# All weight subtractions on VectorE, under a list schedule that knows of the port that VectorE and GpSimd share

## The chip, the cores and the metric

The kernel runs on one core of a Trainium2 chip. Its five engines are TensorE (PE in the views, its weight loads apart as PEld), VectorE (DVE), ScalarE (ACT), GpSimd (POOL) and SyncE (SP), which issues all the DMAs. The metric is the device time of one execution in microseconds, lower being better.

## What is computed

Two transformer-like blocks on 256 tokens of width 1024, all in float32:

```python
h = x
h = h + 0.5 * swiglu(rmsnorm(h), ffn1)                 # 1024 -> 2816 -> 1024
h = h + concat(window_attention(n), gla(n)) @ w_out    # n = rmsnorm(h), one w_in
h = h + 0.5 * swiglu(rmsnorm(h), ffn2)
h = h + sigmoid(rmsnorm(h) @ w_ple) * rmsnorm(p @ w_proj)
for layer in range(2):
    mix = mlstm_and_gated_delta(u) if layer == 0 else hgrn2(u)   # u = rms_norm(h)
    h = h + rms_norm(mix)
    h = h + rms_norm(conv_ffn(rms_norm(h)))            # 1024 -> 2 x 2816 -> 1024
return h
```

The weights are some 200 MB, each is read once, and each is multiplied with all 256 tokens.

## The kernel before

**Three matmuls for one product.** TensorE multiplies in the type float32r. So that little precision is lost, each operand is split in two: `hi` is the operand rounded to float32r, `lo` is the operand minus `hi`. A product is then the sum of three matmuls: x_hi by w_hi, x_lo by w_hi, x_hi by w_lo.

**The weight pipeline** (`halves`, L578 to L600). Weights arrive in half chunks of 128 x 1024 numbers (512 KB). One DMA on SyncE's queue brings a half chunk into one of 3 `raw` buffers. ScalarE rounds it into one of 6 `hi` buffers (L455). Two subtractions of 128 x 512 make the `lo` buffer, also one of 6 (L423). Only when these three have read it is `raw` free for the next DMA, and a `hi` or `lo` buffer is free when the matmuls that read it are done. The string `LOPAT` names the engine of the four subtractions of a chunk, V for VectorE and P for GpSimd.

**The stages.** Most of the time goes to four feed-forward networks. Their inner loop has groups of 256 hidden channels: two chunks of up-weights stand still in TensorE while the tokens move past (96 matmuls of 256 columns, `row_units`), VectorE and ScalarE make the 256 hidden channels (`row_fin`, or `up_fin` with a convolution), and one chunk of down-weights moves past them (24 matmuls of 512 columns, `down`). Between the networks lie three mixers and some normalisations, with chains of small operations.

**What sets the order.** `Plan` records every instruction with its engine, an assumed duration and its operands, and then simulates a list schedule at build time: on each engine the ready instruction with the highest priority goes next, within the buffers that are free (`forward`). A second pass takes its priorities from a schedule that is made backwards from the end. What comes out is one fixed queue for each engine, which the chip then works through in order, with semaphores. The assumed durations are in `tt`, `ts`, `stt`, `act`, `copy` and, for TensorE, in `pec`. So a duration that is changed there changes no instruction, only the queues. In the schedule of before the engines are independent of each other apart from data and buffers.

**What shares an engine with the subtractions.** GpSimd also does the elementwise products with `eng=TTX` (one for each 256 hidden channels, and several in the mixers) and the powers of the normalisations. VectorE does nearly all else that is elementwise.

Of the kernel before, what the change touches and what calls it, by code (L numbers as in the profile page):

```python
# [14 lines left out]
P = 128  # L15
# [33 lines left out]
LOPAT = "VVVP"  # L49
# [16 lines left out]
class Plan:  # L66
    """Records instructions, then issues them in the order of a list schedule: per engine the
    ready instruction with the longest way to the end first, within the tiles that are free.
    Every pair that touches the same bytes, one of them writing, keeps its recorded order."""

    ENGS = ("PE", "ACT", "DVE", "POOL", "SP")
    # from the end of one instruction to the start of one that needs it (ns)
    WAIT = {"PE": (0, 197, 197, 224, 200), "ACT": (260, 143, 142, 170, 200), "DVE": (256, 198, 127, 155, 200),
            "POOL": (203, 75, 60, 96, 200), "SP": (2000,) * 5}
    TICK, TICK_COLS = 3413.0, 3060  # the PE clock is halved after a tick with fewer columns
# [7 lines left out]
    def tile(self, tag, shape, dt=F32, bufs=1, keep=999):  # L83
        """A tile that lives from its first to its last use, in one of the tag's `bufs` places."""
# [47 lines left out]
    def add(self, alts, outs, ins, func=None, cols=0.0):  # L132
        """alts: the ways to do it, each (engine, ns, function that issues it)."""
        i = len(self.ops)
        if self.places is not None:
            self.ops.append(alts)
            return
# [4 lines left out]
        for key, m, q in rd:  # L142
            keys.add(key)
            bank = self.masks[key][1] == 0  # reads of one PSUM bank by two engines do not overlap
            deps.update(j for j, m2, q2, w in self.hist[key]
                        if (w or bank and [x[0] for x in self.ops[j][0]] + engs != 2 * engs[:1]) and m & m2 and q & q2)
# [15 lines left out]
    def order(self):  # L162
        """The best of a few list schedules: the first by the way to the end, the next ones by the
        latest starts of a schedule from the end backwards that prefers what ended last before."""
# [31 lines left out]
    def lat(self, i, j, e=None):  # L196
        """From the end of i (on e) to the start of j."""
        return self.WAIT[e or self.ops[i][0][0][0]][self.ENGS.index(self.ops[j][0][0][0])]

    def backward(self, when):  # L200
        """Latest starts (negative, 0 the end) with each engine doing one thing at a time."""
# [33 lines left out]
    def forward(self, rank, prio):  # L235
# [14 lines left out]
        free = dict.fromkeys(self.WAIT, 0.0)  # L250
        tset = "silu_and_others"
# [3 lines left out]
        def safe(tag, ks):  # L255
            """Whether the rest could still run in recorded order if `ks` got their places now."""
# [13 lines left out]
        def start(i):  # L270
            """Earliest start by data and tiles; None while a tile has no place."""
# [17 lines left out]
        def later(i, e, t):  # L289
            """Whether another engine would be done with i clearly before e."""  # L290
            end = t + next(x[1] for x in ops[i][0] if x[0] == e)
            return any(max(ready[i], free[x[0]]) + x[1] + ALT < end for x in ops[i][0] if x[0] != e)
        for _ in range(n):
            best = None
            for e, c in cand.items():
                el = []
                for i in c:
                    t = start(i)
                    if t is not None and not (len(ops[i][0]) > 1 and later(i, e, max(t, free[e]))):
# [39 lines left out]
            free[e] = fin[i] = t + c  # L339
            when[i] = (t, fin[i])  # L340
# [25 lines left out]
class Kern:  # L366
    def __init__(self, plan, a, tap):
        self.plan, self.nc, self.a, self.tap = plan, plan.nc, a, tap
        self.phase = 0
        self.pieces = PIECES  # of the first load of weights  # L370

# [43 lines left out]
    def tt(self, out, a, b, op, eng="DVE"):  # L415
        n = self.fsz(out)

        def way(eng):
# [4 lines left out]
            return eng, c, lambda: self.ew(eng).tensor_tensor(out=out, in0=a, in1=b, op=op)  # L423
        self.plan.add([way(x) for x in eng.split("|")], [out], [a, b])

    def ts(self, out, a, s1, s2=None, op0=ALU.mult, op1=None, eng="DVE"):
# [5 lines left out]
        self.plan.add([(eng, c, lambda: e.tensor_scalar(out=out, in0=a, scalar1=s1, scalar2=s2, op0=op0, **kw))], [out],  # L432
                      [a] + [x for x in (s1, s2) if hasattr(x, "tensor")])

    def stt(self, out, a, s, b, op0, op1, accum=None):
        self.plan.add([("DVE", 69 + 1.04 * self.fsz(out) + 62 * hasattr(s, "tensor"),
                        lambda: self.nc.vector.scalar_tensor_tensor(out=out, in0=a, scalar=s, in1=b, op0=op0, op1=op1, accum_out=accum))],  # L437
# [19 lines left out]
    def copy(self, out, a, eng=None):  # L457
        n = self.fsz(out)
        ways = {"DVE": ("DVE", 69 + (1.04 if self.ps_(out, a) else 0.53) * n,
                        lambda: self.nc.vector.tensor_copy(out, a)),  # L460
# [21 lines left out]
    def pec(l, r):  # L482
# [6 lines left out]
        if r.dtype == F32:  # L489
            return 2 * max(m / 1.2, 2.5 + n / 1.2), n / 1.2 * 2  # L490
        return max(m / 1.2, 2.5 + n / 2.4), n / 2.4
# [1424 lines left out]
```

## Time and profile before

| | |
|---|---|
| time, median of 3 runs | 1327.42 us (1326.01 to 1330.7) |
| span of the profiled execution, which is the only time known of it | 1328.2 us |
| TensorE matmuls busy | 1263.0 us, 95% |
| VectorE busy | 874.1 us, 66% |
| ScalarE busy | 675.2 us, 51% |
| GpSimd busy | 495.3 us, 37% |
| mean rate of the DMAs | 158 GB/s |

The profile is that of one execution. Busy time counts an instruction from its start to its end, and the ends overlap on pipelined engines, so TensorE at 95% doesn't say that TensorE works at its best rate 95% of the time. [...]

### The profile page before, as it was taken

The page shows a single profiled execution, that of the slowest core. Times are in us where ns is not written, and L with a number is a line of the kernel's source. Part 1 is how long each engine was busy: PE and PEld are TensorE (multiplying, and loading weights), DVE is VectorE, ACT ScalarE, POOL GpSimd, SP SyncE. Part 2 cuts the span into 40 slices and gives each one's busy share as a digit, 9 for nine tenths or more (in the row PEclk, how much of TensorE's full clock was granted, in tenths as well). Part 3 has the DMA queues.
Part 4 walks back from the last instruction along what each step waited for, and adds up shares of the span by engine and source line. Part 5 has one row for each costly group of instructions (what it writes and reads, how often), then busy time and mean ns, then how long its engine had stood idle before and what let it go on. Part 6 is the DMA issues. An engine that isn't in the chain of part 4 may idle for free.

```text
span 1328.2 us, 21657 instructions
## 1 busy us (share of the span) xinstructions
PE 1263.0 (95%) x8180; PEld 1110.6 (84%) x8180; DVE 874.1 (66%) x1434; ACT 675.2 (51%) x1126; POOL 495.3 (37%) x435
## 2 busy tenths in 40 slices
PE   7999999899999999999999989999899999999998
PEld 7899987567889998788877788999699777899896
DVE  5656566766655666759456867666867557766765
ACT  5444445544464344547445565555643255555554
POOL 3433333533243333225213333333334643333332
PEclk9999999899999999999999999999998899999999
DMA  8655554216455555542223554555643045555552
GB/s 277 204 191 181 181 177 144 97 57 203 148 173 175 184 180 186 178 142 68 96 96 111 189 170 162 173 190 180 200 149 128 17 143 174 174 177 188 173 177 98
DMA packets 61034, 209.52 MB, mean 158 GB/s; under 512 B 7409, under 2 KB 9602, under 8 KB 60802
## 3 DMA queue, kind: packets, MB, share of 16 engines
q1 hardware_dynamic: 60930, 208.14, 47.9%
q8 instruction: 64, 1.05, 0.3%
q14 instruction: 40, 0.33, 0.1%
HBM read 207.07 MB, written 1.05 MB: 157 GB/s over the span
## 4 chain that ended last, share of the span: by engine, by line
PE 53%; DVE 18%; DMA 13%; ACT 7%; issue 5%; POOL 4%; SPq 0%; DVEq 0%; ACTq 0%; POOLq 0%
PE psa L496 51%; DVE lo L423 10%; ACT hi L455 5%; DMA raw<-in_cf_u 4%; DMA raw<-in_w_ffn 4%; DVE big L437 3%; POOL lo L423 2%; DMA raw<-in_cf_d 2%; PE psa L507 2%; DVE big L423 2%; DMA raw<-in_w_out 1%; DMA raw<-in_w_ple 1%; DMA raw<-in_w_cB 1%; DVE g L423 1%; POOL sml L423 1%
## 5 line engine op out<-in xcount | busy, mean ns | idle before, releaser
L423 DVE TENSOR_TENSOR lo<-raw,hi 128x512 fp32r<-128x512 f32 (+1 forms) x567 | 469.0, 858 | 277.2 <-ACT hi L455 276.7
L455 ACT ACTIVATE hi<-raw 128x1024 fp32r<-128x1024 f32 x381 | 393.3, 1046 | 392.6 <-PE psa L496 271.9
L423 POOL TENSOR_TENSOR lo<-raw,hi 128x512 fp32r<-128x512 f32 (+1 forms) x189 | 302.5, 1601 | 570.3 <-ACT hi L455 534.0
L496 PE MATMUL psa<-xh,lo 128*128 128x256 f32 x1568 | 449.6, 287 | 12.3 <-DVE lo L423 11.4
L496 PE MATMUL psa<-xh,hi 128*128 128x256 f32 x1568 | 448.5, 286 | 12.0 <-ACT hi L455 9.2
L496 PE MATMUL psa<-xl,hi 128*128 128x256 f32 x1568 | 443.8, 283 | 0.0
L496 PEld LDWEIGHTS psa<-xh,lo 128*128 128x128 f32 x1568 | 298.4, 190 | 21.4 <-DVE lo L423 21.2
L496 PEld LDWEIGHTS psa<-xh,hi 128*128 128x128 f32 x1568 | 298.8, 191 | 20.6 <-ACT hi L455 10.3
L496 PEld LDWEIGHTS psa<-xl,hi 128*128 128x128 f32 x1568 | 298.3, 190 | 7.5 <-DVE xl L437 0.2
L496 PE MATMUL psa<-hi,halfr 128*128 128x512 f32 x720 | 205.9, 395 | 2.5 <-ACT halfr L455 2.0
L496 PE MATMUL psa<-hi,xh 128*128 128x512 f32 (+1 forms) x368 | 146.0, 416 | 1.1 <-ACT xh L455 1.1
L496 PEld LDWEIGHTS psa<-hi,halfr 128*128 128x128 f32 x720 | 124.8, 188 | 23.9 <-ACT halfr L455 3.7
L496 PE MATMUL psa<-lo,xh 128*128 128x512 f32 (+1 forms) x368 | 141.2, 401 | 2.0 <-DVE lo L423 1.9
L496 PE MATMUL psa<-hi,xl 128*128 128x512 f32 (+1 forms) x368 | 139.7, 417 | 3.3 <-DVE xl L423 3.2
L423 POOL TENSOR_TENSOR big<-big 128x256 f32<-128x256 f32 (+1 forms) x88 | 81.4, 926 | 97.5 <-ACT big L455 66.0
L496 PE MATMUL psa<-lo,halfr 128*128 128x512 f32 x360 | 114.0, 393 | 0.6 <-DVE lo L423 0.6
L496 PEld LDWEIGHTS psa<-big,big 128*128 128x128 f32 (+10 forms) x752 | 88.4, 180 | 24.8 <-issue 10.8
L496 PE MATMUL psa<-big,big 128*128 128x128 f32 (+13 forms) x752 | 103.8, 275 | 5.0 <-DVE big L423 2.2
L496 PEld LDWEIGHTS psa<-lo,xh 128*128 128x128 f32 x368 | 71.0, 193 | 19.2 <-DVE lo L423 4.5
L496 PEld LDWEIGHTS psa<-hi,xl 128*128 128x128 f32 x368 | 69.5, 194 | 18.8 <-DVE xl L423 6.8
L496 PEld LDWEIGHTS psa<-hi,xh 128*128 128x128 f32 x368 | 71.0, 193 | 14.8 <-ACT xh L455 2.7
L496 PEld LDWEIGHTS psa<-lo,halfr 128*128 128x128 f32 x360 | 67.6, 188 | 17.4 <-DVE lo L423 2.4
(166 smaller groups left out, 1058.9 us busy)
## 6 DMA issues: line engine op xcount, KB each, us to landing
raw<-in_w_ffn SPq DMA_DIRECT2D x131, 512.0 KB, 4.5
raw<-in_cf_u SPq DMA_DIRECT2D x88, 512.0 KB, 4.1
raw<-in_cf_d SPq DMA_DIRECT2D x44, 512.0 KB, 4.2
raw<-in_w_in SPq DMA_DIRECT2D x16, 512.0 KB, 4.2
raw<-in_w_abB SPq DMA_DIRECT2D x16, 512.0 KB, 4.2
raw<-in_w_cA SPq DMA_DIRECT2D x16, 512.0 KB, 3.9
raw<-in_w_cB SPq DMA_DIRECT2D x16, 512.0 KB, 4.1
raw<-in_w_abA SPq DMA_DIRECT2D x12, 512.0 KB, 4.6
```

What stands on the lines that cost most here:

```text
L423: return eng, c, lambda: self.ew(eng).tensor_tensor(out=out, in0=a, in1=b, op=op)
L437: lambda: self.nc.vector.scalar_tensor_tensor(out=out, in0=a, scalar=s, in1=b, op0=op0, op1=op1, accum_out=accum))],
L455: self.plan.add([("ACT", c, lambda: self.nc.scalar.activation(out, a, f, scale=scale, **kw))], outs, ins, SETS.get(f))
L496: return [self.nc.tensor.matmul(o, l, r, start=st, stop=sp) for o, l, r, st, sp in lst]
L507: self.plan.add([("PE", 2.5 + P / 1.2, lambda: self.nc.tensor.transpose(out, a, idn))], [out], [a, idn], cols=P * 2)
```

## The change

One letter of `LOPAT` moves the last subtraction of each chunk, 189 of 756, from GpSimd to VectorE. In the list schedule each way to do an instruction gets a fourth field: whether it holds the port that VectorE and GpSimd share. It is set for elementwise instructions of two inputs without an operand in PSUM, on either engine, and for VectorE's copies and scalar operations between buffers in SBUF. An instruction with the field set starts, in the simulated schedule, no earlier than the last such instruction ended, on whichever of the two engines. And `pec` and `tp` assume other durations for matmuls: 120 ns where they had 109 for 256 columns of float32r, and 230 where they had 216 for 512 columns. The comments and docstrings of the file are gone as well, and the rest of the text is the same.

```diff
-LOPAT = "VVVP"
+LOPAT = "VVVV"
...
     def add(self, alts, outs, ins, func=None, cols=0.0):
         i = len(self.ops)
+        alts = [x if len(x) == 4 else (*x, False) for x in alts]
...
         free = dict.fromkeys(self.WAIT, 0.0)
+        port = 0.0
...
-            return any(max(ready[i], free[x[0]]) + x[1] + ALT < end for x in ops[i][0] if x[0] != e)
+            return any(max(ready[i], free[x[0]], port if x[3] else 0.0) + x[1] + ALT < end for x in ops[i][0] if x[0] != e)
...
                     t = start(i)
+                    if t is not None and any(x[3] for x in ops[i][0] if x[0] == e):
+                        t = max(t, port)
...
             free[e] = fin[i] = t + c
+            if ops[i][0][way][3]:
+                port = fin[i]
...
-            return eng, c, lambda: self.ew(eng).tensor_tensor(out=out, in0=a, in1=b, op=op)
+            return eng, c, lambda: self.ew(eng).tensor_tensor(out=out, in0=a, in1=b, op=op), op != ALU.pow and not self.ps_(a, b)
...
-        self.plan.add([(eng, c, lambda: e.tensor_scalar(out=out, in0=a, scalar1=s1, scalar2=s2, op0=op0, **kw))], [out],
+        self.plan.add([(eng, c, lambda: e.tensor_scalar(out=out, in0=a, scalar1=s1, scalar2=s2, op0=op0, **kw),
+                        eng == "DVE" and not self.ps_(out, a))], [out],
...
-                        lambda: self.nc.vector.scalar_tensor_tensor(out=out, in0=a, scalar=s, in1=b, op0=op0, op1=op1, accum_out=accum))],
+                        lambda: self.nc.vector.scalar_tensor_tensor(out=out, in0=a, scalar=s, in1=b, op0=op0, op1=op1, accum_out=accum),
+                        not self.ps_(a, b))],
...
-                        lambda: self.nc.vector.tensor_copy(out, a)),
+                        lambda: self.nc.vector.tensor_copy(out, a), not self.ps_(out, a)),
...
         if r.dtype == F32:
-            return 2 * max(m / 1.2, 2.5 + n / 1.2), n / 1.2 * 2
-        return max(m / 1.2, 2.5 + n / 2.4), n / 2.4
+            if l.shape[0] <= 64:
+                return 2 * (m + n) / 1.2, n / 1.2 * 2
+            return 2 * max(4 + m / 1.2, 2.5 + n / 1.2), n / 1.2 * 2
+        return max(4 + m / 1.2, 9.5 + 0.4316 * n), n / 2.4
...
-        self.plan.add([("PE", 2.5 + P / 1.2, lambda: self.nc.tensor.transpose(out, a, idn))], [out], [a, idn],
+        self.plan.add([("PE", 4 + P / 1.2, lambda: self.nc.tensor.transpose(out, a, idn))], [out], [a, idn],
```

The first place where the queues differ in a way that the prediction uses is VectorE in the inner loop of the first feed-forward network. `lo<-raw,hi` is a subtraction of weights, `big<-psa,half` the scaling of 256 new channels from PSUM, `halfr` the low half of those channels. Before, over half a group:

```order
L423 TENSOR_TENSOR big_145<-psa_117,half_110 128x512
L423 TENSOR_TENSOR lo_104<-raw_102,hi_129 128x512 x2
L423 TENSOR_TENSOR halfr_122<-big_143,halfr_121 128x256
L423 TENSOR_TENSOR lo_130<-raw_106,hi_123 128x512
L423 TENSOR_TENSOR lo_119<-raw_114,hi_129 128x512 x2
L423 TENSOR_TENSOR big_146<-psa_137,half_110 128x512
```

And after:

```order
L430 TENSOR_TENSOR big_145<-psa_131,half_110 128x512
L430 TENSOR_TENSOR lo_119<-raw_102,hi_107 128x512 x2
L430 TENSOR_TENSOR halfr_122<-big_143,halfr_121 128x256
L430 TENSOR_TENSOR lo_116<-raw_114,hi_123 128x512 x2
L430 TENSOR_TENSOR lo_104<-raw_106,hi_107 128x512 x2
L430 TENSOR_TENSOR lo_119<-raw_102,hi_107 128x512 x2
L430 TENSOR_TENSOR lo_104<-raw_114,hi_123 128x512 x2
L430 TENSOR_TENSOR halfr_128<-big_144,halfr_127 128x256
```

Subtractions that stood alone, because GpSimd had the other half, are now pairs.

The second place is GpSimd's queue at the same part of the program. Before:

```order
L423 TENSOR_TENSOR lo_130<-raw_102,hi_129 128x512
L423 TENSOR_TENSOR lo_116<-raw_114,hi_103 128x512
L423 TENSOR_TENSOR big_144<-big_144 128x256
L423 TENSOR_TENSOR big_145<-big_145 128x256
L423 TENSOR_TENSOR lo_130<-raw_106,hi_123 128x512
```

And after, where `big<-big` is the product of 256 channels with their gates:

```order
L430 TENSOR_TENSOR big_144<-big_144 128x256
L430 TENSOR_TENSOR big_145<-big_145 128x256
L430 TENSOR_TENSOR big_146<-big_146 128x256
L430 TENSOR_TENSOR big_147<-big_147 128x256
L430 TENSOR_TENSOR big_148<-big_148 128x256
```

The subtractions have left it, and only the products remain there.

The third place is VectorE in the second mixer, where the triangular inverse begins. `c_lmf` and `c_ident` are tables in SBUF, `psa` is PSUM. Before:

```order
L423 TENSOR_TENSOR big_141<-big_111,c_lmf_66 128x512
L423 TENSOR_TENSOR big_90<-c_ident_62,big_91 128x512
L423 TENSOR_TENSOR lo_124<-raw_102,hi_118 128x512
L423 TENSOR_TENSOR big_149<-c_ident_62,psa_131 128x512
L423 TENSOR_TENSOR lo_130<-raw_114,hi_107 128x512
L423 TENSOR_TENSOR big_152<-big_152,psa_105 128x128x2
L423 TENSOR_TENSOR big_142<-c_ident_62,big_141 128x512
```

And after:

```order
L430 TENSOR_TENSOR big_146<-c_ident_62,big_141 128x512
L445 SCALAR_TENSOR_TENSOR big_89<-psa_125,s_15_239,big_132 128x128
L430 TENSOR_TENSOR big_91<-c_ident_62,psa_136 128x512
L445 SCALAR_TENSOR_TENSOR big_89<-psa_125,s_15_239,big_132 128x128 x3
L445 SCALAR_TENSOR_TENSOR big_92<-psa_109,s_15_239,big_151 128x128 x4
L445 SCALAR_TENSOR_TENSOR big_143<-psa_137,s_15_239,big_72 128x128 x4
L430 TENSOR_TENSOR big_91<-big_91,psa_136 128x128x2
L430 TENSOR_TENSOR big_147<-big_89,c_lmf_66 128x512
```

Operations that read PSUM have moved ahead of those with two inputs in SBUF, and the subtractions of weights have moved behind this stretch.

## Rows read from the trace of the kernel before

**Rows 1.** The page: busy time, share of the span and number of instructions of each engine, and the shares of the span on the chain that ended last.

```profile
PE 1263.0 (95%) x8180; PEld 1110.6 (84%) x8180; DVE 874.1 (66%) x1434; ACT 675.2 (51%) x1126; POOL 495.3 (37%) x435
...
PE 53%; DVE 18%; DMA 13%; ACT 7%; issue 5%; POOL 4%; SPq 0%; DVEq 0%; ACTq 0%; POOLq 0%
```

**Rows 2.** The waits of TensorE's weight loads (each matmul has one ahead of it) over the whole span: for whom, us in total, how often, the longest.

```profile
PEld psa L496 <- DVE lo L423: 28.2, 58, 1.4
PEld psa L507 <- DVE big L437: 16.5, 15, 3.7
...
PEld psa L496 <- DVE xl L423: 7.0, 9, 2.0
PEld psa L496 <- POOL lo L423: 4.3, 8, 1.7
```

**Rows 3.** The instructions that write or read the tile `lo`: number, shortest, median and longest in ns; and from the same view who waited for them (us, times).

```profile
L423 DVE TENSOR_TENSOR lo<-raw,hi x567: 426/691/1815, 7.0 to 1310.2; 128x512 fp32r<-128x512 f32 x187, 128x272 fp32r<-128x272 f32 x2
...
L423 POOL TENSOR_TENSOR lo<-raw,hi x189: 773/1741/2347, 11.4 to 1309.8; 128x512 fp32r<-128x512 f32 x187, 128x272 fp32r<-128x272 f32 x2
...
PEld psa L496: 32.5, 66
```

**Rows 4.** Busy time of each engine by stretch: the inner loops of the two gated and the two convolution networks, and in the middle the densest 30 us of the second mixer. Columns: stretch, its length, busy us and number of PE, PEld, DVE, ACT and POOL, the granted clock, the DMA share, GB/s.

```profile
54.40:188.80 134.40, 133.27 (x928) 123.65 (x928) 76.99 (x98) 57.81 (x78) 50.65 (x39) 1.00 0.56 179
400.00:512.00 112.00, 110.34 (x761) 101.85 (x761) 69.11 (x84) 47.63 (x64) 42.37 (x33) 1.00 0.56 181
605.00:635.00 30.00, 24.92 (x188) 22.69 (x188) 29.37 (x67) 18.04 (x33) 21.47 (x15) 0.99 0.22 70
835.00:930.00 95.00, 93.78 (x655) 87.32 (x654) 64.31 (x100) 51.03 (x75) 34.91 (x27) 1.00 0.55 179
1157.00:1290.00 133.00, 130.95 (x906) 120.88 (x906) 91.85 (x148) 71.69 (x108) 49.71 (x39) 1.00 0.53 178
```

**Rows 5.** The same stretches for the instructions on the tile `lo` alone. Columns: stretch, its length, busy us and number of PE, PEld, DVE and POOL, then as above.

```profile
54.40:188.80 134.40, 90.49 (x310) 58.39 (x310) 58.98 (x68) 36.08 (x23) 1.00 0.56 179
400.00:512.00 112.00, 74.27 (x254) 48.34 (x254) 53.05 (x58) 30.12 (x20) 1.00 0.56 181
605.00:635.00 30.00, 8.60 (x28) 5.45 (x29) 8.94 (x8) 3.38 (x2) 0.99 0.22 70
835.00:930.00 95.00, 63.11 (x218) 41.39 (x217) 37.68 (x49) 27.37 (x17) 1.00 0.55 179
1157.00:1290.00 133.00, 88.40 (x304) 56.99 (x303) 60.50 (x67) 33.62 (x23) 1.00 0.53 178
```

**Rows 6.** The waits of the weight loads for `lo` on VectorE, in the four inner loops of rows 4 in order of time.

```profile
PEld psa L496 <- DVE lo L423: 3.2, 9, 0.4
...
PEld psa L496 <- DVE lo L423: 3.8, 9, 1.0
...
PEld psa L496 <- DVE lo L423: 2.4, 6, 0.8
...
PEld psa L496 <- DVE lo L423: 3.4, 8, 0.5
```

**Rows 7.** The timeline at one seam of the second gated network's loop, VectorE, GpSimd and weight loads: start, us from the first start to the last end, the instruction, its number, and the idle time before it with what ended it.

```profile
443.33 1.29 DVE L423 TENSOR_TENSOR lo<-raw,hi 128x512 fp32r<-128x512 f32 x2 [1.02 <-ACT hi L455]
448.18 0.69 DVE L423 TENSOR_TENSOR big<-psa,half 128x512 f32<-128x512 f32 x1 [3.55 <-PE psa L496]
448.79 3.91 DVE L423 TENSOR_TENSOR lo<-raw,hi 128x512 fp32r<-128x512 f32 x3
...
448.53 1.29 POOL L423 TENSOR_TENSOR lo<-raw,hi 128x512 fp32r<-128x512 f32 x1 [5.07 <-ACT hi L455]
...
449.82 0.19 PEld L496 LDWEIGHTS psa<-xl,hi 128*128 128x128 f32 x1
450.42 0.19 PEld L496 LDWEIGHTS psa<-xh,lo 128*128 128x128 f32 x1 [0.41 <-DVE lo L423]
```

**Rows 8.** The timeline in the second mixer, VectorE and then GpSimd, with the same columns.

```profile
620.88 1.20 DVE L423 TENSOR_TENSOR big<-big,c_lmf 128x512 f32<-128x512 f32 x1
622.00 1.76 DVE L423 TENSOR_TENSOR big<-c_ident,big 128x512 f32<-128x512 f32 x1
623.69 1.75 DVE L423 TENSOR_TENSOR lo<-raw,hi 128x512 fp32r<-128x512 f32 x1
628.73 3.44 DVE L423 TENSOR_TENSOR lo<-raw,hi 128x512 fp32r<-128x512 f32 x2
...
618.54 11.41 POOL L423 TENSOR_TENSOR big<-big,c_lmf 128x512 f32<-128x512 f32 x7
629.90 3.38 POOL L423 TENSOR_TENSOR lo<-raw,hi 128x512 fp32r<-128x512 f32 x2
```

**Rows 9.** Two more of VectorE's operations with two inputs in SBUF: number, shortest, median and longest in ns (by tile), and for `halfr` the busy us, the mean ns and the idle time before (by form).

```profile
L437 DVE SCALAR_TENSOR_TENSOR c_h<-big,sml,c_h x16: 740/746/1797, 738.9 to 1324.4; 128x512 f32<-128x512 f32 x16
...
L423 DVE TENSOR_TENSOR halfr<-big,halfr x88: 409/422/1527, 31.9 to 1314.8; 128x256 fp32r<-128x256 f32 x88
...
L423 DVE TENSOR_TENSOR halfr<-big,halfr 128x256 fp32r<-128x256 f32 x88 | 62.7, 713 | 5.1 <-ACT halfr L455 2.7 <-PE psa L496 2.0
```

**Rows 10.** The chain that ended last, two pieces of it in the first 50 us: start, us, what.

```profile
45.40 1.81 POOL lo L423
47.23 5.24 DMA raw<-in_w_ffn
```

## The prediction, made before the changed kernel ran

> **What bounds the kernel now.** The page comes first: TensorE is busy for 95% of the span, VectorE for 66%, GpSimd for 37%, and the chain that ended last runs through TensorE for 53% and through VectorE for 18% [rows 1]. So time can only come out of places where TensorE stands still, and VectorE is the engine most often behind that. The waits of the weight loads say for what: 28.2 us for a weight subtraction on VectorE, 4.3 us for one on GpSimd, 16.5 us for `big` and 7.0 us for `xl`, both of VectorE [rows 2]. The view of the tile `lo` gives the first two as one sum, 32.5 us in 66 waits, and it shows why: a subtraction on VectorE takes 691 ns in the median and up to 1815, and one on GpSimd 773 at least and 1741 in the median [rows 3]. The same work has two durations, and the timeline shows what makes them. At 443.33 two of VectorE's subtractions run alone and take 1.29 us, 0.65 us each. At 448.53 GpSimd begins one of 1.29 us. VectorE's next three begin at 448.79, and take 3.91 us where 1.95 would do [rows 7]. The first of them comes too late for TensorE: the weight load at 450.42 has waited 0.41 us for `lo` [rows 7]. `big<-psa`, which reads PSUM, takes its 0.69 us while GpSimd is at work. So two instructions with both inputs in SBUF, one on each engine, don't run together.
>
> **What the change does to VectorE's load.** 189 subtractions come to it, 189 x 0.65 = 123 us. In the four inner loops, 83 of them (23 + 20 + 17 + 23) bring 54 us. In the same loops VectorE now spends 210.2 us on 242 subtractions, which at 0.65 would be 157.3, so 53 us of it is blocked time [rows 5]. Nearly all of that must be due to GpSimd's subtractions, because they are 127 of the 178 us that GpSimd works there [rows 4, 5]. Further, `halfr` has a mean of 713 ns and a median of 422, another 88 x 0.29 = 26 us over the span [rows 9]. VectorE's busy time therefore stays within some 25 us of its 874, while GpSimd's falls by 300. In the first place that the change shows, a pair takes 1.3 us from the end of `hi`, and before, the second half was done after 1.29 to 1.8 us on GpSimd with VectorE's half blocked beside it.
>
> [...]
>
> **The terms of the sum.**
>
> Inner loops: the weight loads wait 3.2 + 3.8 + 2.4 + 3.4 = 12.8 us for `lo` there [rows 6], and TensorE is busy for all but 6.1 of the 474.4 us [rows 4], so little else is late in them. (The matmuls' modelled ends overlap the waits, which is why 6.1 is less than 12.8; between the two weight loads of rows 7 lie 0.60 us, so the wait is real time.) Each wait is under 0.5 us as a rule, and the block ahead of it 0.6 to 1.1 us. I take 11 us out; bounds 0 (the wait goes to something else) and 12.8.
>
> `lo` waits elsewhere: 32.5 - 12.8 = 19.7 us [rows 3, 6]. There a late DMA or a full VectorE queue can lie behind the same row. I take half, 10 us; bounds 4 and 16.
>
> The second mixer from 605 to 635 us: VectorE is busy for 29.37 of 30 us and TensorE stands still for 5.1 [rows 4]. GpSimd's seven products with `c_lmf` fill 11.41 us without a gap, and VectorE's operations meanwhile take 1.20, 1.76 and 1.75 us in place of about 0.69; behind them two of GpSimd's subtractions block two of VectorE's for 3.44 - 1.29 = 2.15 us [rows 8]. The products stay on GpSimd. But the new queue puts operations that read PSUM beside them, and has the subtractions behind. I take 3 us; bounds 0 and 5.1.
>
> The start: GpSimd's subtraction of 1.81 us is what frees a `raw` buffer for the next DMA at 47.23 [rows 10], and a pair would free it 0.5 us sooner. With three buffers in turn this counts once in some three refills. I take 1 us; bounds 0 and 2.
>
> VectorE's other late results: `c_h` takes 746 ns in the median and 1797 at worst [rows 9], and TensorE waits 16.5 + 7.0 us for `big` and `xl` [rows 2] at the ends of the stages. I take 2 us; bounds 0 and 5.
>
> Cost: 189 - 83 = 106 subtractions land on VectorE outside the loops, 69 us of work that used to lie on another queue. An instruction queued behind one waits 0.65 us more. If one in 20 stands ahead of an operation that TensorE waits for, that is 5 x 0.65 = 3 us; bounds 0, and 18 us for one in four.
>
> The new matmul durations cost nothing in themselves, since no matmul changes. They move the queues, as the port does: in a seam such as that of rows 7 either queue may be better by some tenths of a microsecond. I take 0, with 5 us to either side.
>
> Sum: -11 - 10 - 3 - 1 - 2 + 3 = -24 us on the profiled span of 1328.2, which is 0.8 above the median of the runs. On 1327.4 that gives 1303.4; I say **1304 us**, with a range of its own of 1293 to 1316.
>
> **The rivals.**
>
> *A larger gain.* The schedule has known nothing of blocked ports, so its queues were made for times that didn't hold. With true times the seams of the stages could close, too: half of the 23.5 us for `big` and `xl` go, where I took 2. That is 10 us more, 1294, and with all terms at their good bounds (12.8 + 16 + 5.1 + 2 + 5 = 41) 1286. Against it: most of those waits end chains of normalisation in which each step needs the one before.
>
> *The wait moves on.* A `lo` that is earlier uncovers the next limit, the `hi` buffers that TensorE's own progress frees, or the refill of `raw`. Then the loops give 3 of 12.8 us and the rest of the sum a third, 8 us in all: 1319. For it speaks that DMA has 13% of the chain [rows 1]; against it, that in the loops the rows name `lo` and little else.
>
> *No change.* TensorE's busy time is its work and the waits overlap with matmuls still under way: 1327, within 4 us. (0.3%, 4 us, is about what a measurement of this kernel can tell from no change.) Against it stands that gap of 0.60 us in rows 7.
>
> *Slower.* VectorE becomes the engine that is late. Its place is the mixers and the stage ends, where subtractions meet VectorE's own chains, as between 605 and 635 us, where it is full already [rows 4]. The price is 0.65 us for each one that stands ahead of the chain. The sum without the cost term is -27, so it turns when 42 of the 106 do; at 50 of them, with 32 us of cost, the time is 1332. Against it, the blocked time that goes is as large as the work that comes, and the plan ranks a subtraction by its own due time; the third place that the change shows has them behind the chain.
>
> [...]
>
> **How the numbers follow.** Forecast 0.55, larger gain 0.13, the wait moves on 0.11, no change 0.07, slower 0.14. Faster by over 0.3% is the first three, 0.79; within 0.3% is 0.07; slower 0.14. The range runs from the best bound, 1286, to 1326: this leaves out the slower rival, most of no change and little of the rest, 2 in 10.
>
> **What would show it.** Right: VectorE's `lo` is 756 instructions with a mean near 0.7 us and few over 1.3; VectorE's busy time is 850 to 900 us and GpSimd's near 195; the weight loads' waits for `lo` fall from 32.5 to some 10 us; a 30 us stretch at the triangular inverse has TensorE standing still for less than 5.1 us. Wrong: the waits for `lo` fall and those for `hi`, for DMAs or for `big` and `xl` rise by as much; or `lo` stays long, because what remains on GpSimd blocks it just as well; or VectorE's queue holds `big`, `xl` or `halfr` back behind subtractions at the stage ends.

## The result, and the profile after

The changed kernel takes 1287.39 us in the median of four runs (1276.25 to 1292.31), the kernel before 1326.72: a ratio of 0.9699, with a 95% interval from 0.9648 to 0.9751. The forecast was 1304 in a range of 1286 to 1326. So it went the way that was forecast, by 39 us where 24 were summed up.

The runs of one kernel differ with the granted clock of TensorE: of 11 runs of the kernel before, the fastest took 1318.79 us at a mean clock of 0.994 and the slowest 1334.22 at 0.975. The profiled run of the changed kernel is its fastest (1276.25 us at 0.992; its slowest, 1292.31, had 0.978), and that of the kernel before had 0.984. The 53.7 us between the two spans, 1328.2 and 1274.5, are therefore 14 us more than the medians show, and each size below that is taken from traces leans the same way. The 39 us between the medians owe nothing to the clock: the median of the mean clocks is 0.9825 in the four runs of the change and 0.984 in the 11 of before.

The page after, the lines that answer to [rows 1]:

```profile
PE 1239.4 (97%) x8180; PEld 1102.2 (86%) x8180; DVE 858.0 (67%) x1623; ACT 674.8 (53%) x1126; POOL 201.4 (16%) x246
...
PE 76%; DVE 8%; DMA 7%; ACT 5%; issue 3%; POOL 1%; SPq 0%; DVEq 0%; ACTq 0%; POOLq 0%
```

VectorE does 189 more instructions in 16 us less, and its part of the chain fell from 18% to 8%. The tile `lo`, as in [rows 3]:

```profile
L430 DVE TENSOR_TENSOR lo<-raw,hi x756: 430/685/1793, 7.0 to 1258.2; 128x512 fp32r<-128x512 f32 x187, 128x272 fp32r<-128x272 f32 x2
...
PEld psa L507: 8.5, 24
```

The weight loads wait 8.5 us for it where they waited 32.5. The other waits of [rows 2]:

```profile
PEld psa L507 <- ACT hi L464: 12.0, 8, 7.0
PEld psa L518 <- DVE big L445: 8.9, 6, 4.9
PEld psa L507 <- DVE lo L430: 8.5, 24, 0.6
PEld psa L507 <- DVE xl L430: 4.5, 8, 1.8
```

These rows of `big` and `xl` have lost 10.1 of 23.5 us, and `hi`, on which the rival of the moved wait rested, stands at 12.0 (10.7 before), of which 7.0 is the start of the program. In [rows 2] only the largest row of `big` was taken. The others of before, from the same view, were:

```profile
PEld psa L507 <- DVE big L423: 4.1, 4, 2.9
...
PEld psa L496 <- POOL big L423: 3.6, 4, 1.7
PEld psa L496 <- DVE big L423: 3.0, 2, 2.7
...
PEld psa L496 <- DVE big L432: 1.7, 2, 1.2
```

With five more below 1 us (0.7, 0.5, 0.4, 0.3, 0.2) they come to 14.5 us, of which 3.6 are for GpSimd and 1.2 for ScalarE. After the change all rows of `big` beside the one above come to 3.7 us, so another 10.8 went there.

The inner loops, as in [rows 4] (stretch, length, busy us and number of PE, PEld, DVE, ACT and POOL, the clock, the DMA share, GB/s):

```profile
52.00:186.00 134.00, 134.00 (x950) 126.05 (x949) 78.03 (x123) 59.15 (x78) 14.16 (x16) 1.00 0.56 184
365.00:498.00 133.00, 133.00 (x941) 125.04 (x940) 77.16 (x126) 58.99 (x80) 17.68 (x18) 1.00 0.56 185
800.00:890.00 90.00, 90.00 (x643) 84.77 (x642) 63.88 (x112) 47.53 (x73) 9.71 (x11) 1.00 0.57 186
1130.00:1240.00 110.00, 108.79 (x757) 100.64 (x756) 74.38 (x140) 59.94 (x90) 15.58 (x13) 1.00 0.56 185
```

In the first three TensorE doesn't stop at all, and does 7.09 matmuls per us in the first, where it did 928 / 134.4 = 6.90 before. And the seam of a loop, as in [rows 7], on VectorE:

```profile
418.51 0.68 DVE L430 TENSOR_TENSOR big<-psa,half 128x512 f32<-128x512 f32 x1
420.36 0.42 DVE L430 TENSOR_TENSOR halfr<-big,halfr 128x256 fp32r<-128x256 f32 x1 [1.17 <-PE psa L507]
420.70 0.68 DVE L430 TENSOR_TENSOR big<-psa,half 128x512 f32<-128x512 f32 x1
421.38 2.50 DVE L430 TENSOR_TENSOR lo<-raw,hi 128x512 fp32r<-128x512 f32 x4
```

Four subtractions take 2.50 us, where three took 3.91.

**Where the time went.** The last writes of the residual `h` cut the program into its stages. The four feed-forward networks together went from 819.2 to 806.6 us between the two traces, the three mixers from 484.4 to 444.3. So the networks gave 13 us, where the sum had 11 for their inner loops, and the mixers 40, where the sum had at most the other 13. The first and the third mixer, before (same columns as the loops):

```profile
212.80:343.90 131.10, 123.49 (x623) 94.27 (x622) 83.47 (x159) 66.11 (x136) 45.62 (x49) 0.96 0.38 123
953.90:1126.80 172.90, 165.37 (x1069) 144.03 (x1068) 110.16 (x180) 74.22 (x138) 78.49 (x88) 0.95 0.39 125
```

And after:

```profile
211.90:327.50 115.60, 114.22 (x604) 88.45 (x603) 82.62 (x172) 65.58 (x136) 26.89 (x36) 1.00 0.41 135
918.20:1074.90 156.70, 154.68 (x1064) 135.78 (x1064) 105.87 (x199) 75.07 (x138) 46.36 (x68) 0.99 0.41 136
```

TensorE's idle time went from 7.6 and 7.5 us to 1.4 and 2.0, which is 11.7 of the 31.7 us by which the two are shorter. The rest is matmuls that take less time: TensorE is busy for 9.3 us less in the first, with 19 matmuls fewer, and for 10.7 less in the third, with five fewer. Of that the clock can be 12 us at most, an estimate from the lengths and the mean clocks of these two tables: 0.04 x 131.1 + 0.05 x 172.9 - 0.01 x 156.7. Where the clock reads 0.50, from 569.5 to 572.8 us before, two matmuls of 512 columns begin 0.43 us apart, and 0.23 us apart in the median at the full clock. Parts of the two stretches had these mean clocks before, 0.74 and 0.53:

```profile
1015.00:1048.00 33.00, 30.51 (x206) 27.55 (x204) 25.94 (x47) 4.65 (x9) 20.74 (x31) 0.74 0.20 66
241.50:252.50 11.00, 10.17 (x28) 6.33 (x30) 5.33 (x10) 3.96 (x7) 7.46 (x13) 0.53 0.43 144
```

Since the timed runs of the two kernels have nearly the same mean clock, these 12 us belong to the 14 by which the traces differ more than the medians. And the new queue moved matmuls from one kind of stage to the other: 2861 began in the mixers before and 2834 after, 5236 in the networks before and 5261 after. At 0.15 us each (1239.4 us / 8180) that is 4 us. Without these and the clock the mixers gave some 24 us and the networks some 17.

### The profile page after: what moved, and what is told of

It reads as the page before. It is cut to its first block, busy times and chain, and to the rows that moved or that the text cites. A ratio compares the mean times of both kernels' runs of the same rounds, so it can differ in the third digit from the quotient of the medians.

```text
span 1274.5 us, 21523 instructions
## 1 busy us (share of the span) xinstructions
PE 1239.4 (97%) x8180; PEld 1102.2 (86%) x8180; DVE 858.0 (67%) x1623; ACT 674.8 (53%) x1126; POOL 201.4 (16%) x246
## 4 chain that ended last, share of the span: by engine, by line
PE 76%; DVE 8%; DMA 7%; ACT 5%; issue 3%; POOL 1%; SPq 0%; DVEq 0%; ACTq 0%; POOLq 0%
PE psa L507 73%; DVE lo L430 4%; ACT hi L464 3%; DMA raw<-in_cf_u 3%; PE psa L518 2%; DVE big L445 2%; DMA raw<-in_w_ffn 2%; ACT big L464 1%; DMA raw<-in_w_in 1%; ACT junkACT L464 1%; POOL sml L430 1%; DMA big<-in_xT 0%; DVE big L430 0%; DMA raw<-in_w_out 0%; DMA raw<-in_w_ple 0%
## 5 line engine op out<-in xcount | busy, mean ns | idle before, releaser
L430 DVE TENSOR_TENSOR lo<-raw,hi 128x512 fp32r<-128x512 f32 (+1 forms) x756 | 509.3, 716 | 307.4 <-ACT hi L464 305.4
L507 PE MATMUL psa<-hi,halfr 128*128 128x512 f32 x720 | 212.7, 395 | 2.4 <-ACT halfr L464 1.5
L430 POOL TENSOR_TENSOR big<-big 128x256 f32<-128x256 f32 (+1 forms) x88 | 86.5, 984 | 595.5 <-ACT big L464 490.2
L507 PEld LDWEIGHTS psa<-hi,halfr 128*128 128x128 f32 x720 | 121.8, 189 | 18.0 <-DVE halfr L430 2.2
L507 PEld LDWEIGHTS psa<-big,big 128*128 128x128 f32 (+10 forms) x752 | 80.0, 166 | 19.2 <-issue 9.7
L507 PE MATMUL psa<-big,big 128*128 128x128 f32 (+12 forms) x752 | 95.1, 260 | 0.6 <-DVE big L430 0.5
L464 ACT ACTIVATE big<-big 128x256 f32<-128x256 f32 (+1 forms) x103 | 44.8, 437 | 62.3 <-DVE big L445 30.7
```

The costliest lines, as they stand in the source:

```text
L464: self.plan.add([("ACT", c, lambda: self.nc.scalar.activation(out, a, f, scale=scale, **kw))], outs, ins, SETS.get(f))
L507: return [self.nc.tensor.matmul(o, l, r, start=st, stop=sp) for o, l, r, st, sp in lst]
```

## The experiments

The change has three parts: the letter of `LOPAT`, the port in the schedule, and the durations that the schedule assumes for matmuls. There were two theories at first. **A**: the gain is the blocked time that goes when GpSimd has no subtractions. **B**: it is the schedule that keeps VectorE and GpSimd apart in the mixers, so that TensorE has no long gaps there and keeps its clock. That gaps cost the clock was an assumption of theory B: before, TensorE stands still from 239.84 to 242.33 us and the clock reads 0.50 from 242 to 251 us, but no run shows that the one makes the other. And the port is the schedule's word, in which the traces show only that some instructions take longer side by side: a subtraction on VectorE 0.68 us in the median with GpSimd idle, and 1.58 us when it begins during one on GpSimd (before). Each ratio is to runs of the kernel before that were taken with the experiment. Their median is 1326.09 us in the first four experiments, 1331.68 in the next four and 1322.34 in the last four, so sizes are compared by ratios.

### The letter alone

```diff
-LOPAT = "VVVP"
+LOPAT = "VVVV"
```

> Only the letter of LOPAT: all 756 subtractions on VectorE, the schedule knows nothing of the port and has the old matmul durations. Theory A (the gain is the blocked time that goes when GpSimd has no subtractions): most of the 39 us, time 1295 to 1303, weight loads wait under 12 us for lo. Theory B (the gain is the schedule that keeps VectorE and GpSimd apart in the mixers, so that TensorE has no long gaps and keeps its clock): 10 to 15 us, 1312 to 1317, and the first and third mixer stay within 4 us of their 131 and 173 us.

Measured: 1287.94 us, a ratio of 0.9713 (0.9674 to 0.9752). That is as much as the whole change, and more than theory A said. The weight loads' waits for `lo`:

```profile
PEld psa L503: 5.8, 15
```

They fell by 26.7 us, 19 of them in the networks, and the networks from 819.2 to 792.5 us. Theory A holds there. In the mixers:

```profile
208.00:330.50 122.50, 117.78 (x619) 92.09 (x618) 86.73 (x176) 68.01 (x141) 26.33 (x37) 1.00 0.40 132
916.10:1085.20 169.10, 165.00 (x1068) 143.39 (x1067) 109.42 (x199) 73.92 (x137) 47.88 (x68) 0.95 0.39 128
```

The first lost 8.6 us, the third only 3.8, and it keeps its clock of 0.95.

### The port alone

```diff
+            if ops[i][0][way][3]:
+                port = fin[i]
```

> Only the port in the schedule; a quarter of the subtractions stays on GpSimd and the matmul durations are the old ones. Theory A: 1315 to 1325, because VectorE and GpSimd can be kept apart only by letting one wait in the schedule. Theory B: 1295 to 1305, with 25 us or more out of the two mixers.

Measured: 1284.06 us, a ratio of 0.968 (0.9645 to 0.9714). Theory A was wrong on this by 30 us and more. The mixers:

```profile
206.90:323.50 116.60, 113.95 (x613) 90.95 (x612) 84.38 (x159) 66.54 (x138) 45.10 (x50) 1.00 0.42 139
923.60:1085.00 161.40, 154.99 (x1063) 137.03 (x1064) 104.09 (x180) 73.67 (x136) 77.45 (x87) 0.98 0.40 133
```

They lose 14.5 and 11.5 us with all of GpSimd's 189 subtractions still there (77.45 us of GpSimd in the third, as before), and the clock of the third rises to 0.98. That is the 25 us that theory B had for the two mixers. The clock has little of it, since the timed runs have 0.9865 in the median beside 0.984 before. But the time is 11 us below theory B's range, too, because the networks also fell, from 819.2 to 797.7 us, and the waits for `lo` from 32.5 to 14.7. And the two engines are not kept apart, as theory B has it. The subtractions on VectorE and GpSimd here (busy us, mean ns, idle time before):

```profile
L430 DVE TENSOR_TENSOR lo<-raw,hi 128x512 fp32r<-128x512 f32 x561 | 450.1, 834 | 240.2 <-ACT hi L464 238.8
...
L430 POOL TENSOR_TENSOR lo<-raw,hi 128x512 fp32r<-128x512 f32 x187 | 295.5, 1581 | 531.4 <-ACT hi L464 510.1 <-PE psa L505 13.7 <-issue 4.7
```

And before:

```profile
L423 DVE TENSOR_TENSOR lo<-raw,hi 128x512 fp32r<-128x512 f32 x561 | 466.1, 862 | 276.0 <-ACT hi L455 275.4
...
L423 POOL TENSOR_TENSOR lo<-raw,hi 128x512 fp32r<-128x512 f32 x187 | 300.9, 1610 | 561.9 <-ACT hi L455 525.6 <-DMA raw<-in_w_cB 12.5 <-PE psa L496 9.0
```

Their means are only 28 and 29 ns shorter, so most of the blocked time is still there, and TensorE waits less for it. That a schedule which counts the port gains this much is shown; how its order does it is not.

### The letter and the port

```diff
-            if l.shape[0] <= 64:
-                return 2 * (m + n) / 1.2, n / 1.2 * 2
-            return 2 * max(4 + m / 1.2, 2.5 + n / 1.2), n / 1.2 * 2
-        return max(4 + m / 1.2, 9.5 + 0.4316 * n), n / 2.4
+            return 2 * max(m / 1.2, 2.5 + n / 1.2), n / 1.2 * 2
+        return max(m / 1.2, 2.5 + n / 2.4), n / 2.4
```

This is the change without the third part (`tp` has its old duration, too).

> LOPAT and the port together, with the old matmul durations: what the new durations are worth is the distance to 1287. Both theories: 1283 to 1293. If the durations count, 1298 or more.

Measured: 1269.95 us, a ratio of 0.9574 (0.954 to 0.9609). Neither theory had that: by the medians the kernel is 17 us faster than the changed one. Part of this goes with the clock, which has a median of 0.991 in these runs: at 0.992 the change took 1276.25 us and this kernel 1268.94, so 7 us stay at one clock. Whether the queues or chance made the clock of the change's four runs lower isn't settled. The letter (0.9713) and the port (0.968) would give 0.940 if they were independent. They share some of their gain, and the new durations take 0.005 to 0.0125 of the time back.

### The old queues, issued on VectorE

```diff
-            return eng, c, lambda: self.ew(eng).tensor_tensor(out=out, in0=a, in1=b, op=op)
+            return eng, c, lambda: self.ew(on or eng).tensor_tensor(out=out, in0=a, in1=b, op=op)
```

with `on="DVE"` for the weight subtractions.

> The schedule of before, unchanged (it takes the fourth subtraction for one of GpSimd's with GpSimd's duration), but the 189 instructions are issued on VectorE at the place that they have in the whole order. It separates the blocked time from any better plan. Theory A: 1300 to 1310. Theory B: 1320 or more, since the queues of before are kept; slower than before if the subtractions come ahead of VectorE's chains.

Measured: 1301.79 us, a ratio of 0.9828 (0.9789 to 0.9868). The plan doesn't know of the move, and still 24 us go. Waits for `lo` and the third mixer:

```profile
PEld psa L496: 6.4, 16
```

```profile
924.00:1096.70 172.70, 167.72 (x1071) 147.15 (x1070) 107.97 (x200) 73.99 (x138) 45.25 (x68) 0.93 0.38 125
```

The networks are at 792.0 us, as with the letter in the plan, so there the gain comes from the move itself and not from a better order. The move also replaces GpSimd's subtractions, which take 1.28 us even with VectorE idle (the one at 250.47 us before), by shorter ones, and the experiment doesn't separate this from the blocked time. But of the waits before, 28.2 us name a subtraction on VectorE and 4.3 one on GpSimd [rows 2], so the blocked time is probably most of it. The third mixer is where it was before (172.9), at a clock of 0.93 after 0.95, though GpSimd has 33 us less to do in it. So what is late there is probably the order. That the subtractions would come ahead of VectorE's chains, as in the slower rival, didn't show in the time even where no plan kept them out.

### The durations alone, and each part taken out of the change

The durations alone are the changed kernel with `LOPAT = "VVVP"` and without the line `port = fin[i]`, so that only `pec` and `tp` differ from before in what the plan does.

> Only the new matmul durations, with LOPAT VVVP and a schedule that knows nothing of the port. Theory C (they shift the queues for the worse whatever else holds, by about the 17 us by which LOPAT and the port without them beat the change): 1335 to 1350. Theory D (they are only another queue, with an effect that depends on the rest): anywhere from 1310 to 1335.

Measured: 1376.04 us, a ratio of 1.036 (1.033 to 1.0391). It is the only kernel of this study that is slower than before, by 48 us, more than either theory had. The weight loads wait 62.2 us for `lo`, and VectorE waits longer for `hi`, which was 276.7 us before:

```profile
PEld psa L505: 62.2, 92
```

```profile
DVE lo L428 <- ACT hi L462: 332.9, 206, 4.7
```

The change without the port (its line `port = fin[i]` taken out):

> The change without the port in its schedule. If the port is worth in the new queue what it is worth beside LOPAT alone (18 us): 1305. Theory D: 1285 to 1300.

Measured: 1301.43 us, a ratio of 0.9787 (0.9752 to 0.9822). The port is worth 12 us here (0.9787 to 0.9699), where the first expectation had 18.

The change without the letter (`LOPAT = "VVVP"`):

> The change without the letter of LOPAT. If the letter is worth what it is worth beside the port alone (14 us): 1301. Theory C: 1297 to 1305. Theory D: 1280 to 1297.

Measured: 1322.98 us, a ratio of 0.9947 (0.9922 to 0.9972), far beyond what either expectation had. The letter is worth 33 us here.

With these the eight combinations are complete. Ratios to the kernel before:

| | old durations | new durations |
|---|---|---|
| neither | 1 | 1.036 |
| letter | 0.9713 | 0.9787 |
| port | 0.968 | 0.9947 |
| letter and port | 0.9574 | 0.9699 (the change) |

By the medians the new durations cost time in each row, from 0.007 to 0.036 (in the last row less at one clock, as said above), and least where the subtractions are on VectorE. In the row of the letter the two intervals touch, so the 0.007 is not clear of noise by itself; at a clock of 0.986 the runs there took 1289.62 us with the old durations, and 1296.54 and 1300.75 with the new. So theory C holds in that the durations are for the worse in every row, but not in its size of 17 us, which depends on the rest.

### The new queues, with GpSimd's part back on GpSimd

The opposite of the experiment with the old queues: the plan of the change, but `on="POOL"` for the fourth subtraction of each chunk.

> The queues of the change, but the fourth subtraction of each chunk is issued on GpSimd at its place in the whole order: the blocked time alone, in the new plan. If the blocked time is worth what moving it was worth in the old queues (24 us): 1311. If the new queues are better than the old ones only as long as the plan's picture holds, it falls back to the time of before, 1320 to 1335.

Measured: 1314.89 us, a ratio of 0.9895 (0.9853 to 0.9937), 0.0196 above the change. The move of the subtractions, and the blocked time with it, is worth some 26 us in the new queues, and 23 in the old ones. The networks rise from 806.6 to 825.9 us and the waits for `lo` from 8.5 to 27.7.

### What the new durations do

The question left was why durations that are closer to the trace make worse queues: before, at the full clock, matmuls of 256 columns begin 0.12 us apart in the median and those of 512 columns 0.23, which the new durations (120 and 230 ns) meet. Theory **F**: taking the float32r matmuls for longer, the plan rounds the weights later, and less margin is left. Theory **G**: it is the mixers' matmuls and transposes.

The change with the old float32r durations, and the new ones for the rest:

```diff
-        return max(4 + m / 1.2, 9.5 + 0.4316 * n), n / 2.4
+        return max(m / 1.2, 2.5 + n / 2.4), n / 2.4
```

> The change with the old assumed durations for the float32r matmuls alone (109 and 216 ns); the transposes and the float32 matmuls keep the new ones. Theory F (what costs the 17 us is that the plan, taking the float32r matmuls for longer, puts the rounding of weights later, so that less margin is left before TensorE wants them): 1267 to 1275, weight loads wait 6 us or less for lo. Theory G (the mixers' matmuls do it): 1282 to 1292.

The letter and the port with this line as in the change, and the old durations for the rest:

> The other half: only the float32r matmuls have the new durations (120 and 230 ns), transposes and float32 matmuls the old ones. Theory F: 1282 to 1292. Theory G: 1267 to 1275.

Measured: 1272.44 us with the old float32r durations (0.9627, from 0.9594 to 0.966), 1275.85 with the new ones alone (0.965, from 0.9618 to 0.9682). On top of 0.9574 that is 0.005 for one half and 0.008 for the other, and the intervals overlap, so the medians don't decide between F and G, and 1275.85 is nearer to what G expected. At a clock of 0.992, though, the new float32r durations alone took 1275.85 us and the whole change 1276.25, so beside them the other half costs nothing there. All three kernels have a clock of 0.991 to 0.993 in the median, so it isn't that. The traces tell the halves apart. VectorE's waits for the rounded weights, with old and then with new float32r durations:

```profile
DVE lo L430 <- ACT hi L464: 232.7, 175, 4.8
```

```profile
DVE lo L430 <- ACT hi L464: 306.3, 197, 4.8
```

The networks take 790.6 and 805.4 us, and the weight loads wait 4.9 and 13.0 us for `lo`. In the change itself the same three numbers are 305.4, 806.6 and 8.5. So in the networks the loss comes with the float32r durations. Some of it is only work that moved: with them 5274 matmuls begin in the networks where 5244 did, some 4 us, and the mixers take 446.9 us where they took 451.5. VectorE's waits alone don't say that the weights are late, but the landings do: in the networks a half chunk's rounding begins, in the mean, 1.28 us after it has landed with the letter and the port, 1.25 with the old float32r durations, and 1.49 and 1.47 with the new ones and in the change. So the rounding is later, as F has it, though by 0.2 us only. What the other half costs in the medians stays open; its mixers (456.0 us against 451.5 without it) would account for 4 us.

The other side of F, float32r durations 8 per cent below the old ones, which are already below the new:

```diff
-        return max(m / 1.2, 2.5 + n / 2.4), n / 2.4
+        return 0.92 * max(m / 1.2, 2.5 + n / 2.4), n / 2.4
```

> LOPAT and the port, and matmul durations of float32r another 8 per cent below the old ones (100 and 199 ns), which are below what the trace shows. Theory F: the weights are prepared earlier still, 1262 to 1270, or 1270 if the margin was enough already. If the old durations were better by chance only: 1275 or more.

Measured: 1255.55 us, a ratio of 0.9491 (0.9459 to 0.9524). It is the fastest kernel of the study, some 28 us below the change by the ratios, and below what F had. Its page:

```profile
PE 1220.2 (97%) x8180; PEld 1095.3 (87%) x8180; DVE 867.3 (69%) x1623; ACT 673.8 (54%) x1128; POOL 198.6 (16%) x246
...
PEclk9999999999999999999999999999999999999999
```

The clock was granted in full nearly throughout (a mean of 0.999 here, 0.996 at least in the other runs), and the networks are at 785.0 us. But the weights are not earlier than with the letter and the port, as F has it: the rounding begins 1.30 us after the landing (1.28 there), VectorE waits 236.4 us for `hi` (233.5), and the weight loads wait 4.6 us for `lo` (5.4). The mean clocks of the two traces are 0.999 and 0.990, and 0.009 of 1269 us is 11 of the 15.6 us between their spans. So this run doesn't show that more margin helps. A queue that happens to leave the clock up is the rival, and it isn't ruled out.

And the change as it is, with 3.5 us instead of 2 assumed from the end of a transfer to its reader (the plan counts 1.5 us for the transfer of 512 KB, so it has 5.0 us from issue to reader here and 3.5 elsewhere):

```diff
-            "POOL": (203, 75, 60, 96, 200), "SP": (2000,) * 5}
+            "POOL": (203, 75, 60, 96, 200), "SP": (3500,) * 5}
```

> The change as it is, with one other number: the schedule assumes 3.5 us instead of 2 us from a DMA to its reader, so it loads earlier. Theory F, if the margin that is missing is that of the DMAs, which land 4.3 to 4.5 us after their issue: 1268 to 1278. If the margin is lost behind the DMA, in the queue of ScalarE: 1283 to 1292.

Measured: 1267.47 us, a ratio of 0.9579 (0.9546 to 0.9612). With the new durations kept, one number that makes the loads earlier brings the kernel to where it is without them (0.9574), at a clock of 0.994 in the median (at 0.993 it took 1266.7 us, 10 less than the change at 0.992). VectorE's waits for the rounded weights and the weight loads' for `lo` fall from 305.4 and 8.5 us:

```profile
DVE lo L430 <- ACT hi L464: 267.7, 172, 5.0
```

```profile
PEld psa L507 <- DVE lo L430: 5.8, 17, 0.9
```

The networks are at 789.4 us, and the rounding begins 1.33 us after the landing where it was 1.47. The page of the change has, from issue to landing:

```profile
raw<-in_w_ffn SPq DMA_DIRECT2D x131, 512.0 KB, 4.5
```

So a plan with 3.5 us from issue to reader is 1 us short. That fits a plan in which margin between a DMA and the matmuls was missing, and in which the shorter durations had supplied it without saying so. It isn't more than a fit: the waits for `lo` fell by 2.7 us only, and what makes up the rest of the 17 us of the networks stays open.

## Why the prediction was right, and where it was off

**The blocked time was right, with its size.** That the two engines' subtractions don't run together was read from [rows 7], and the whole trace of before has it: 130 of GpSimd's 187 of 128x512 begin while one of VectorE's is under way and end 1.15 us after it in the median, and 100 of VectorE's begin during one of GpSimd's and end 0.55 us after it. With the subtractions on one engine the blocked time went: `halfr` has a mean of 443 ns after 713 [rows 9], and the longest `c_h` is 753 ns after 1797. In the four loops VectorE is busy for 219.0 us with 324 subtractions, 8 more than at 0.65 us each, where it was 53 more. GpSimd's products still block a few: the longest subtraction takes 1.79 us, and begins 0.34 us after a product of 1.58 us on GpSimd (at 702.63). VectorE's busy time was to be 850 to 900 us and is 858.0, GpSimd's near 195 and is 201.4.

**The inner loops** were to give 11 us. The weight loads there waited 12.8 us for `lo` [rows 6] and now wait 2.0 us, all of it in the last loop.

**The `lo` waits elsewhere** were to give 10 of 19.7 us. In all, `lo` waits fell by 24.0, so 13 of them did.

**The second mixer's dense stretch** was to give 3 of 5.1 us. The stretch that answers to it, after the change:

```profile
590.00:620.00 30.00, 29.10 (x230) 27.36 (x229) 24.44 (x63) 18.16 (x33) 17.58 (x14) 1.00 0.27 91
```

TensorE stands still for 0.9 us, 4.2 less, so the term was a little low. The rows that answer to [rows 8] show what was given as the reason, first VectorE and then GpSimd:

```profile
595.34 1.12 DVE L430 TENSOR_TENSOR big<-big,c_lmf 128x512 f32<-128x512 f32 x1
596.49 0.69 DVE L430 TENSOR_TENSOR big<-c_ident,big 128x512 f32<-128x512 f32 x1
597.09 0.34 DVE L445 SCALAR_TENSOR_TENSOR big<-psa,s,big 128x128 f32<-128x128 f32 x1
597.36 0.68 DVE L430 TENSOR_TENSOR big<-c_ident,psa 128x512 f32<-128x512 f32 x1
597.95 1.89 DVE L445 SCALAR_TENSOR_TENSOR big<-psa,s,big 128x128 f32<-128x128 f32 x7
...
597.29 11.29 POOL L430 TENSOR_TENSOR big<-big,c_lmf 128x512 f32<-128x512 f32 x8
```

While GpSimd does its products, VectorE at first runs operations that read PSUM, and one of 128x512 takes 0.68 us beside them. But that this is the cause is not shown. The same stretch, from 13.5 us before the first product to 16.5 after it, with the letter alone and with the port alone:

```profile
578.40:608.40 30.00, 25.57 (x183) 23.69 (x182) 29.23 (x63) 16.23 (x27) 21.09 (x14) 0.96 0.31 104
```

```profile
582.76:612.76 30.00, 25.16 (x192) 23.96 (x191) 28.52 (x74) 17.73 (x32) 22.93 (x17) 0.91 0.18 60
```

TensorE stands still for 4.4 and 4.8 us there, and for 3.1 with both and the old durations. With the port alone VectorE, too, starts with operations that read PSUM, and then has four subtractions beside GpSimd's products:

```profile
603.43 6.78 DVE L430 TENSOR_TENSOR lo<-raw,hi 128x512 fp32r<-128x512 f32 x4
```

So the plan's knowledge of the port doesn't close this stretch by itself, and what does in the change stays open.

**VectorE's other late results** were the step that failed most: 2 us, bounded by 5. The two rows that I read lost 10.1 us, and the other rows of `big`, which I didn't read, another 10.8. In all the waits for `lo`, `big` and `xl` fell by 24.0 + 20.9 = 44.9 us between the traces, where the sum had 11 + 10 + 3 + 2 = 26 for them. Not all of them were time: by the pages TensorE's idle time fell from 65.2 to 35.1 us. The rival of the larger gain had priced the two rows at half of 23.5 us, and was nearer. One reason why such chains are late was in the prediction: VectorE's operations at 1.20 to 1.76 us in place of 0.69 beside GpSimd [rows 8]. I had used that for one stretch of 30 us. How much of the other waits it explains no experiment shows.

**The port in the schedule** had no term of its own beside those 3 us. Alone it takes 42 us (0.968), as much as the letter alone (0.9713). The rival of the larger gain had its effect, seams that close under true times, and gave it 10 us.

**The durations were not worth zero.** "I take 0, with 5 us to either side" is the step that failed: they cost 7 to 17 us beside the other two parts, and 48 alone. My argument was that no matmul changes. The queues do, and of all numbers in the plan this one scales the time that TensorE is thought to need, and so the time by which a weight has to be ready. The plan's other figures kept their own errors: it allows 3.5 us from the issue of a DMA to its reader, and the page has a median of 4.5 us to the landing alone.

**The cost term** of 3 us for subtractions in front of VectorE's chains doesn't show in these traces. With the old queues on VectorE, where such a cost should be largest, the mixers lost 9 us instead.

So 1304 was 17 us too high because VectorE's other late results and the port in the schedule were priced far too low, while the durations, put at nothing, took some of that back. That the result lies inside the range is partly luck, since these two errors have opposite signs: with the letter and the port alone the kernel is at 1270, below the range.

## What to carry to other kernels

When a planner gets better numbers, test each number by itself: a figure nearer to the trace can make a worse schedule, as it would if it removes a margin that covered another figure's error. A plan that counts which instructions of two engines take longer side by side can be worth as much as moving work off one of the two (0.968 against 0.9713), even where most collisions stay. So look in the trace at what a better plan really changed, and not at what it was written to change. And the waits for a tile are to be summed over all rows that name it before its term is bounded: here the small rows of `big` gave 10.8 us, and the two rows that were read 10.1.

## What was not expected of the hardware

The same program's time moves with the granted clock by 15 us of 1326 (1318.79 us at 0.994, 1334.22 at 0.975), and between the queues the clock differs: its mean over each timed run is between 0.978 and 0.992 for the change, between 0.989 and 0.994 for the letter and the port, and between 0.996 and 0.999 for the fastest kernel, with the same 8180 matmuls. If all that is missing from the full clock was spent at 0.50, as the view from 242 to 251 us before has it, that was some 42 us of the profiled execution before and some 20 after, an estimate from the mean clocks of 0.984 and 0.992. None of the 39 us between the medians comes from this: at one mean clock, 0.984, runs of the kernel before took 1324.09 and 1326.09 us and one of the changed kernel 1286.76.
